# Conv taps handed out behind the projections' banks, and the conv normalisation as a step behind the last projection

## The chip, the cores and the metric

The kernel runs on one core of a Trainium2 chip, as one launch. The metric is the device time of one execution in microseconds. The core's engines each work through their own instruction stream in order: PE multiplies matrices, DVE and POOL work on vectors, ACT evaluates functions and makes scaled copies, SP's queue issues DMAs. An instruction that waits holds up all that stands behind it on its engine.

## The reference, cut to what matters

One layer over 1024 tokens of width 1024, all in float32. One projection of the normalised input feeds three groups of heads, whose outputs are joined, projected and added to the input; a gated feed-forward network follows.

```python
h = rms_norm(x, norm_mix[i])
proj = h @ w_in[i]
p_conv, p_nsa, p_rwkv = jnp.split(proj, splits, axis=-1)
y_conv = conv_mixer(p_conv, ...)
y_nsa = nsa_mixer(p_nsa, ...)
y_rwkv = rwkv7_mixer(p_rwkv, ...)
mix = jnp.concatenate([y_conv, y_nsa, y_rwkv], axis=-1)
x = x + mix @ w_out[i]
...
def conv_mixer(p, dw_w, dw_b, ln_g, ln_b):
    u, gate = jnp.split(p, 2, axis=-1)
    y = u * jax.nn.sigmoid(gate)
    y = causal_dwconv(y, dw_w, dw_b)     # 31 taps, 256 channels
    y = layer_norm(y, ln_g, ln_b, LN_EPS)
    return jax.nn.silu(y)
```

The attention group has compressed, selected and windowed keys. The RWKV group is a recurrence over the tokens, done in chunks, each of which needs a small triangular system solved.

## The kernel before, in words

Float32 products are made of three matmuls: both factors are split into a high and a low part, and `mm3` (L229) issues high by high, high by low and low by high. A weight block arrives by DMA as `wraw`; ACT writes its high part `whi` (L120) and DVE the difference `wlo` (L121). `proj_T` makes one block of 128 projection columns: two halves of 512 tokens, 24 matmuls each into one PSUM bank, and a `consume` function that reads the bank.

A framework puts the engines' instructions in order before the run: it takes them in program order as their priority and moves one ahead where an engine would otherwise wait. Steps of the recurrence are issued at high priority. Stage 1 is written by a string of steps:

```python
steps="lora r0 S00 conv taps V00 S01 keys q C00 V01 r1a cmp0 r1b cmp1 r1c S10 C01 V10 S11 C10 V11 C11"
```

`lora`, `r0`, `r1a` to `r1c` are projections for the recurrence (two pairs of heads, 0 and 1), `conv` those of the convolution (its gated input is `cy`, written at L257), `keys` and `q` those of the attention, `cmp0` and `cmp1` the compressed keys. S, V and C with two digits are the recurrence for a pair of heads and a half of the tokens:

- S prepares the operands (L430 to L478 on DVE, L446 and L474 on PE), multiplies them (L493, masked by DVE at L497 into `GA` and `GR`), sends `GA` through DRAM (`dn`, L503, and back into `sN`, L506), and then solves small triangular systems on POOL: 31 pairs of a product `sx` (L528) and a sum into `sT` (L530). DVE copies the result transposed (`sTT`, L532), and SP stores both (`dt`, `dtt`, L534 and L535). The next substitution begins with a copy into `sT` (L523), which must wait for those stores.
- V loads the result (`DF`, L543) and completes the solution with small matmuls (L550 and on).
- C walks through the eight chunks, each needing the state of the one before: L591, L596, L609 and L611 on PE, with DVE's work between them.

`taps` is `conv_rest`: 31 taps over two halves of 128 channels. For the first half DVE makes each tap in one instruction of 128x1024 (L270 for the first, L272 for the others, accumulator `cacc`). For the second half ACT scales (`ctap`, L278) and POOL adds (L274, L279), in pieces of 512 tokens. Behind the taps stands the layer normalisation over channels, for each half of the tokens: sums over partitions by matmuls (L284, L294, L303, into `tr` banks), DVE and ACT work, and four stores to `md` (L311).

Behind stage 1 comes the attention, first on POOL with copies of `kcmp`, `vcmp`, `gates` and `cval` (L669) and masks (L661, L663). Each of its tiles loads queries (`q`, L826, and `QS`, L831 and L832) and begins with matmuls on `kcmp` (L839) and on the keys (L893, L894); L918 are its first transposes.

Of the kernel before, what the change touches and what calls it, by code (L numbers as in the profile page):

```python
# [10 lines left out]
AF = mybir.ActivationFunctionType  # L11
ALU = mybir.AluOpType
AX = mybir.AxisListType
PSUM = bass.MemoryType.PSUM
T = 1024
D = 1024
P = 128


class K:  # L20
    def __init__(self, tc, a, out, ctx, bufs=None):
# [3 lines left out]
                      mm=3, tr=2, av=1, rw=2, mm1=2, tr1=2, pm=2, early="00 01", ga=2, gb=1, gc=1, y=16, r4=15, ta=3, tb=4, mid=2, de=dict(S3="gpsimd", T3="vector", T1="gpsimd", T2="gpsimd", T4="vector", S1="gpsimd", S2="gpsimd", S4="gpsimd"), order=(7, 6, 5, 4, 0, 3, 2, 1), sc=0, pk=1280, st="sync", last=5, sub="gpsimd",  steps="lora r0 S00 conv taps V00 S01 keys q C00 V01 r1a cmp0 r1b cmp1 r1c S10 C01 V10 S11 C10 V11 C11", both=0, cm="gpsimd", rpu=(), wo="vector", tap=(0, 31), vt="cv", vs="vector", va={1: (0, 1), 3: (2, 3), 5: (4, 5), 7: (6, 7)}, vq="sync", vl=1, vw=1, t1=("pm", "tr1"), into={6: (6, 2), 4: (4, 2), 3: (3, 1), 2: (2, 1), 1: (1, 1), 0: (0, 1)})  # L25
# [209 lines left out]
    def proj_T(self, cols, hT, consume, n=P, tag="mm1", halves=(0, 1)):  # L235

        hi, lo = self.wload(cols if isinstance(cols, list) else [cols], n)
        for half in halves:
            pt = self.bank(tag)
            self.mm3(pt[:n], [(hi[k], lo[k], hT[0][half][k], hT[1][half][k]) for k in range(8)])  # L240
            consume(half, pt)

# [17 lines left out]

    def conv_rest(self):
        nc = self.nc
        acc = [self.t4(name="cacc")[:, 0:T] for _ in range(2)]
        for j in range(2):
            y, t = self.cy[j], acc[j]
            m = self.B["tap"][j]
            for d in range(31):
                w = self.cw[:, j, d:d + 1]
                if d >= m and d == 0:
                    nc.vector.tensor_scalar(t, y[:, 0:T], w, self.cb[:, j:j + 1], op0=ALU.mult, op1=ALU.add)  # L270
                elif d >= m:
                    nc.vector.scalar_tensor_tensor(t, y[:, d:d + T], w, t, op0=ALU.mult, op1=ALU.add)  # L272
                elif d == 0:
                    nc.gpsimd.tensor_scalar(t, y[:, 0:T], w, self.cb[:, j:j + 1], op0=ALU.mult, op1=ALU.add)  # L274
                else:
                    for o in (0, 512):
                        z = self.xt([P, 512], "cv", name="ctap")
                        nc.scalar.activation(z, y[:, o + d:o + d + 512], AF.Copy, scale=w)  # L278
                        nc.gpsimd.tensor_tensor(t[:, o:o + 512], t[:, o:o + 512], z, op=ALU.add)  # L279
        for half in range(2):  # L280
            sl = slice(half * 512, half * 512 + 512)
            pm = self.bank("tr1")
# [21 lines left out]
            for j in range(2):  # L304
                z = self.xt([P, 512], "cv", name="cz")
# [967 lines left out]
    def build(self):  # L1273
        order = self.B["order"]
        nc, a = self.nc, self.a
# [7 lines left out]
        hT = self.T_tiles("hT", (self.x, "hx", self.B["hx"]))  # L1283
# [21 lines left out]
        us = {}  # L1305

# [9 lines left out]
        def chain(j, h):  # L1316
            with self.tc.high_priority(offset=100000):
                self.rwkv_chain(us[j, h])
        steps = dict(lora=lambda: self.rwkv_lora(hT), keys=lambda: self.attn_keys(hT), q=lambda: self.attn_q(hT),
                     cmp=lambda: self.attn_cmp(hT), conv=lambda: self.conv_proj(hT), taps=self.conv_rest, r0=lambda: self.rwkv_proj(0, hT),  # L1320
                     r1=lambda: self.rwkv_proj(1, hT), cmp0=lambda: self.attn_cmp(hT, (0,)), cmp1=lambda: self.attn_cmp(hT, (1,)),
                     r1a=lambda: self.rwkv_proj(1, hT, (0,)), r1b=lambda: self.rwkv_proj(1, hT, (1,)), r1c=lambda: self.rwkv_proj(1, hT, (2,)))
# [80 lines left out]
```

## Time and profile before

| | us |
|---|---|
| median of the three runs shown | 1532.06 |
| lowest and highest of them | 1527.68, 1541.17 |
| the profiled execution, its own time | 1533.06 |
| span of its trace | 1531.3 |

The profiled execution lies 1.00 us above the median, and 1.8 us of it lie outside the span. In the trace stage 1 ends at about 385 us, the attention and its surroundings fill the time to about 715, the output projection to about 835, and the feed-forward network the rest. All positions below are microseconds from the start of the span.

### The profile page before, as it was taken

How to read it: one execution, taken by the hardware profiler on the slowest of the kernel's cores; microseconds unless marked ns; L12 is line 12 of the kernel's file. 1: busy time of each engine (PE TensorE's matmuls, PEld its weight loads, DVE VectorE, ACT ScalarE, POOL GpSimd, SP SyncE). 2: the span in 40 equal slices, each digit the busy share in tenths (PEclk: the TensorE clock that was granted, in tenths of full speed). 3: DMA queues.
4: the chain of work that ended last, by engine and by line, in shares of the span. 5: the costliest groups of instructions: out<-in, count | busy, mean ns of one | idle time of the engine just before them, and what ended most of it. 6: DMA issues, size and time to landing. Idle time of an engine off the chain costs nothing.

```text
span 1531.3 us, 22605 instructions
## 1 busy us (share of the span) xinstructions
PE 1431.6 (93%) x8025; PEld 1135.8 (74%) x8025; DVE 1042.6 (68%) x2193; ACT 684.2 (45%) x1361; POOL 488.6 (32%) x585
## 2 busy tenths in 40 slices
PE   6999679999799999998899999999999999897897
PEld 5887457777677777775687788888888887685686
DVE  6247695453586778587267767767767668979976
ACT  6432354534266567677133534334433333343453
POOL 1004887910420050001001223323323315849820
PEclk9999787989799999999999999999999999998999
DMA  6142223433710112114522122222222229163302
GB/s 188 37 120 56 52 83 87 144 93 108 193 32 15 32 39 64 55 39 129 179 90 76 55 69 83 89 77 83 77 89 83 67 93 375 43 203 121 117 1 110
DMA packets 182916, 143.41 MB, mean 94 GB/s; under 512 B 53715, under 2 KB 143124, under 8 KB 182804
## 3 DMA queue, kind: packets, MB, share of 16 engines
q1 hardware_dynamic: 182804, 141.98, 30.5%
q8 instruction: 63, 1.03, 0.3%
q14 instruction: 49, 0.40, 0.1%
HBM read 103.92 MB, written 38.01 MB: 93 GB/s over the span
## 4 chain that ended last, share of the span: by engine, by line
PE 75%; DVE 11%; DMA 5%; POOL 3%; issue 2%; ACT 1%; SPq 1%; DVEq 0%; POOLq 0%; ACTq 0%
PE mm L229 13%; PE gb L229 12%; PE ga L229 9%; PE rw L229 8%; PE gc L229 8%; PE tr L918 5%; PE av L926 4%; DVE sp L121 4%; PE tr L229 3%; PE mm L893 2%; PE mm L894 2%; POOL sT L530 1%; POOL sx L528 1%; PE pm L493 1%; DVE cacc L272 1%
## 5 line engine op out<-in xcount | busy, mean ns | idle before, releaser
L229 PE MATMUL mm<-hT,whi 128*128 128x512 f32 x608 | 204.8, 418 | 0.0
L229 PE MATMUL mm<-hT,wlo 128*128 128x512 f32 x304 | 127.8, 422 | 20.3 <-DVE wlo L121 20.3
L229 PEld LDWEIGHTS mm<-hT,whi 128*128 128x128 f32 x608 | 120.2, 200 | 29.4 <-issue 1.6
L1050 POOL TENSOR_TENSOR S<-wraw,wr 128x512 f32<-128x512 f32 x22 | 28.5, 1297 | 257.9 <-DVE or L107 96.1
L921 ACT ACTIVATE pT<-tr 128x512 f32<-128x512 f32 (+1 forms) x152 | 80.0, 537 | 62.6 <-PE tr L918 61.3
L926 PE MATMUL av<-pT,V 128*64 128x128 f32 x1056 | 95.2, 286 | 4.0 <-ACT pT L921 3.9
L279 POOL TENSOR_TENSOR cacc<-cacc,ctap 128x512 f32<-128x512 f32 x60 | 91.1, 1542 | 17.7 <-ACT ctap L278 17.5
L229 PE MATMUL rw<-sp,sp 128*128 128x512 f32 x330 | 90.0, 397 | 7.1 <-DVE sp L121 6.6
L918 PE MATMUL tr<-idn,pp 128*128 128x128 f32 x528 | 89.6, 288 | 0.1
L229 PEld LDWEIGHTS mm<-hT,wlo 128*128 128x128 f32 x304 | 60.8, 200 | 38.6 <-DVE wlo L121 21.4
L229 PE MATMUL tr<-sp,sp 128*128 128x512 f32 x330 | 88.4, 395 | 0.0
L229 PE MATMUL rw<-woh,mix 128*128 128x512 f32 x240 | 78.9, 405 | 6.4 <-DVE xn L976 5.2
L926 PEld LDWEIGHTS av<-pT,V 128*64 128x64 f32 x1056 | 59.2, 136 | 28.9 <-issue 11.0
L229 PEld LDWEIGHTS rw<-sp,sp 128*128 128x128 f32 x330 | 62.6, 191 | 22.6 <-DVE sp L121 8.8
L893 PE MATMUL mm<-KH,QS 128*128 128x512 f32 (+2 forms) x192 | 74.1, 394 | 4.0 <-DMA QS<-qd 2.5
L918 PEld LDWEIGHTS tr<-idn,pp 128*128 128x128 f32 x528 | 55.7, 141 | 28.6 <-issue 27.3
L121 DVE TENSOR_TENSOR sp<-b,sp 128x512 fp32r<-128x512 f32 x60 | 65.5, 1104 | 13.4 <-ACT sp L120 13.3
L229 PEld LDWEIGHTS tr<-sp,sp 128*128 128x128 f32 x330 | 63.1, 191 | 13.4
L849 POOL TENSOR_TENSOR cmp<-cmp,cmx 128x512 f32<-128x512 f32 (+7 forms) x8 | 5.4, 680 | 206.2 <-DVE cmx L847 137.0
L120 ACT ACTIVATE whi<-wraw 128x512 fp32r<-128x512 f32 x55 | 34.6, 628 | 78.7 <-PE mm L229 60.3
L121 DVE TENSOR_TENSOR wlo<-wraw,whi 128x512 fp32r<-128x512 f32 x55 | 42.3, 771 | 34.9 <-ACT whi L120 34.8
L528 POOL TENSOR_TENSOR sx<-sN,sT 128x60 f32<-128x60 f32 (+24 forms) x124 | 43.8, 353 | 65.4 <-DMA sN<-dn 57.0
(460 smaller groups left out, 3846.3 us busy)
## 6 DMA issues: line engine op xcount, KB each, us to landing
wr<-in_ffn_w_gate_dram SPq DMA_DIRECT2D x44, 256.0 KB
wraw<-in_ffn_w_up_dram SPq DMA_DIRECT2D x44, 256.0 KB
pd<-prod SPq DMA_DIRECT2D x44, 256.0 KB
ta<-pd SPq DMA_DIRECT2D x33, 256.0 KB
wraw<-in_w_in_dram SPq DMA_DIRECT2D x30, 256.0 KB
tb<-in_ffn_w_down_dram SPq DMA_DIRECT2D x22, 256.0 KB
rb<-in_ffn_w_down_dram SPq DMA_DIRECT2D x20, 256.0 KB
qd<-ev SPq DMA_DIRECT2D x16, 256.0 KB
```

Of the source, the lines that this page charges most:

```text
L120: self.nc.scalar.activation(hi, src, AF.Copy)
L121: getattr(self.nc, eng).tensor_tensor(lo, src, hi.bitcast(F32), op=ALU.subtract)
L229: mm = lambda l, r, **k: self.nc.tensor.matmul(out, l, r, skip_group_check=more, **k)
L272: nc.vector.scalar_tensor_tensor(t, y[:, d:d + T], w, t, op0=ALU.mult, op1=ALU.add)
L279: nc.gpsimd.tensor_tensor(t[:, o:o + 512], t[:, o:o + 512], z, op=ALU.add)
L528: v_.tensor_tensor(x, N[:, q, q + 1:32].unsqueeze(2).to_broadcast([P, n, w]), Tm[:, q, 0:w].unsqueeze(1).to_broadcast([P, n, w]), op=ALU.mult)
L893: pe.matmul(pts[g][:, 0:n], QS[:, r, g, :], KH[g][hf][:, ks], start=True, stop=False)
L894: pe.matmul(pts[g][:, 0:n], QS[:, r, g, :], KL[g][hf][:, ks], start=False, stop=True)
L918: pe.transpose(pt[:, o:o + P], Ps[g][:, kt * P:kt * P + P], self.idn)
L921: s.activation(pT[:, 0:n], pt[:, 0:n], AF.Copy)
L926: pe.matmul(av[g * 64:g * 64 + 64, r * P:r * P + P], self.V[kk // 2][:, kk % 2, vo + g * 64:vo + g * 64 + 64], pT[:, o:o + P], start=first ...
L1050: gp.tensor_tensor(t, x, y, op=op)
```

## The change

The taps of both channel halves become a list `self.fill` of 62 small functions. `proj_T` calls up to three of them behind each `consume`, that is, behind each bank of every projection that follows `taps` in the string. What is left of the list is called at the new step `cend`, which then does the normalisation. `cend` stands behind `r1c` and ahead of S10; the normalisation stood within `taps`. Each of the list's functions has the same instructions as before; the two channel halves now alternate, the second first. Line numbers behind `proj_T` grow by 3 and behind the taps by 11: the copy `sTT` at L532 is L543 after, the substitution at L528 and L530 is L539 and L541, L669 is L680, L839 is L850, L550 is L561, the taps at L270 and L272 are L273 and L275.

```diff
@@ -22,7 +22,7 @@
...
-                      steps="lora r0 S00 conv taps V00 S01 keys q C00 V01 r1a cmp0 r1b cmp1 r1c S10 C01 V10 S11 C10 V11 C11", both=0,
+                      steps="lora r0 S00 conv taps V00 S01 keys q C00 V01 r1a cmp0 r1b cmp1 r1c cend S10 C01 V10 S11 C10 V11 C11", both=0, drip=3,
...
@@ -239,6 +239,9 @@
             pt = self.bank(tag)
             self.mm3(pt[:n], [(hi[k], lo[k], hT[0][half][k], hT[1][half][k]) for k in range(8)])
             consume(half, pt)
+            for _ in range(self.B["drip"]):
+                if self.fill:
+                    self.fill.pop(0)()
 
 
     def conv_proj(self, hT):
@@ -258,25 +261,33 @@
             self.proj_T(w[:, j * P:(j + 1) * P], hT, cu)
             self.cy.append(y)
 
+    def conv_taps(self):
+
+        nc = self.nc
+        self.cacc = [self.t4(name="cacc")[:, 0:T] for _ in range(2)]
+
+        def tap(d, j):
+            y, t, w = self.cy[j], self.cacc[j], self.cw[:, j, d:d + 1]
+            if d >= self.B["tap"][j]:
+                if d == 0:
+                    nc.vector.tensor_scalar(t, y[:, 0:T], w, self.cb[:, j:j + 1], op0=ALU.mult, op1=ALU.add)
+                else:
+                    nc.vector.scalar_tensor_tensor(t, y[:, d:d + T], w, t, op0=ALU.mult, op1=ALU.add)
+            elif d == 0:
+                nc.gpsimd.tensor_scalar(t, y[:, 0:T], w, self.cb[:, j:j + 1], op0=ALU.mult, op1=ALU.add)
+            else:
+                for o in (0, 512):
+                    z = self.xt([P, 512], "cv", name="ctap")
+                    nc.scalar.activation(z, y[:, o + d:o + d + 512], AF.Copy, scale=w)
+                    nc.gpsimd.tensor_tensor(t[:, o:o + 512], t[:, o:o + 512], z, op=ALU.add)
+        self.fill = [lambda d=d, j=j: tap(d, j) for d in range(31) for j in (1, 0)]
+
     def conv_rest(self):
         nc = self.nc
-        acc = [self.t4(name="cacc")[:, 0:T] for _ in range(2)]
-        for j in range(2):
-            y, t = self.cy[j], acc[j]
-            m = self.B["tap"][j]
-            for d in range(31):
-                w = self.cw[:, j, d:d + 1]
-                if d >= m and d == 0:
-                    nc.vector.tensor_scalar(t, y[:, 0:T], w, self.cb[:, j:j + 1], op0=ALU.mult, op1=ALU.add)
-                elif d >= m:
-                    nc.vector.scalar_tensor_tensor(t, y[:, d:d + T], w, t, op0=ALU.mult, op1=ALU.add)
-                elif d == 0:
-                    nc.gpsimd.tensor_scalar(t, y[:, 0:T], w, self.cb[:, j:j + 1], op0=ALU.mult, op1=ALU.add)
-                else:
-                    for o in (0, 512):
-                        z = self.xt([P, 512], "cv", name="ctap")
-                        nc.scalar.activation(z, y[:, o + d:o + d + 512], AF.Copy, scale=w)
-                        nc.gpsimd.tensor_tensor(t[:, o:o + 512], t[:, o:o + 512], z, op=ALU.add)
+        for f in self.fill:
+            f()
+        self.fill = []
+        acc = self.cacc
         for half in range(2):
             sl = slice(half * 512, half * 512 + 512)
             pm = self.bank("tr1")
@@ -1303,6 +1314,7 @@
         self.attn_params()
         g2 = self.g2
         us = {}
+        self.fill = []
 
         def start(j, h):
             with self.tc.high_priority(offset=100000):
@@ -1317,7 +1329,7 @@
             with self.tc.high_priority(offset=100000):
                 self.rwkv_chain(us[j, h])
         steps = dict(lora=lambda: self.rwkv_lora(hT), keys=lambda: self.attn_keys(hT), q=lambda: self.attn_q(hT),
-                     cmp=lambda: self.attn_cmp(hT), conv=lambda: self.conv_proj(hT), taps=self.conv_rest, r0=lambda: self.rwkv_proj(0, hT),
+                     cmp=lambda: self.attn_cmp(hT), conv=lambda: self.conv_proj(hT), taps=self.conv_taps, cend=self.conv_rest, r0=lambda: self.rwkv_proj(0, hT),
                      r1=lambda: self.rwkv_proj(1, hT), cmp0=lambda: self.attn_cmp(hT, (0,)), cmp1=lambda: self.attn_cmp(hT, (1,)),
                      r1a=lambda: self.rwkv_proj(1, hT, (0,)), r1b=lambda: self.rwkv_proj(1, hT, (1,)), r1c=lambda: self.rwkv_proj(1, hT, (2,)))
         for st in self.B["steps"].split():
```

On DVE, around the copy `sTT` of S00 (L532), the taps (L272) stand ahead of it before:

```order
L272 SCALAR_TENSOR_TENSOR cacc_1587<-cy_1389,par,cacc_1587 128x1024 x3
L424 SCALAR_TENSOR_TENSOR cum_2032<-rst,lw_2025 128x512
L272 SCALAR_TENSOR_TENSOR cacc_1587<-cy_1389,par,cacc_1587 128x1024
L432 TENSOR_SCALAR lw_2025<-rk_2015,par 128x512
L430 COPY rPC_2038<-Pt_2034 128x8
L461 TENSOR_TENSOR rP_2078<-rr_2016,Pt_2034 128x512
L257 SCALAR_TENSOR_TENSOR cy_1521<-ev_1455,mm_279_1535 128x512
L272 SCALAR_TENSOR_TENSOR cacc_1587<-cy_1389,par,cacc_1587 128x1024
L532 COPY sTT<-sT 128x256
L121 TENSOR_TENSOR wlo_2255<-wraw_2252,whi_2254 128x512
```

The same place of DVE after, from the write of `cy` (L260) that precedes `sTT` (L543) to the first tap (L273):

```order
L260 SCALAR_TENSOR_TENSOR cy_1521<-ev_1455,mm_279_1535 128x512
L543 COPY sTT<-sT 128x256
L121 TENSOR_TENSOR wlo_1931<-wraw_1928,whi_1930 128x512
L450 TENSOR_SCALAR rn_305_1723<-pm_1718 128x8
L106 TENSOR_SCALAR rs_t_307_1726<-rn_305_1723 128x8
L109 TENSOR_SCALAR rs_h_308_1729<-rn_305_1723 128x8
L107 TENSOR_SCALAR rrn_1725<-rs_t_307_1726 128x8
L260 SCALAR_TENSOR_TENSOR cy_1521<-ev_1456,mm_280_1561 128x512
L114 TENSOR_TENSOR rs_t_307_1726<-rrn_1725 128x8
L121 TENSOR_TENSOR wlo_1937<-wraw_1934,whi_1936 128x512
L273 TENSOR_SCALAR cacc_1587<-cy_1389,par 128x1024
```

All of the taps that stood ahead of `sTT` (15, with the first at L270) stand behind it now, from the first on; the 31 of them end among the weights of `q`, before those of the recurrence.

On POOL, at the end of stage 1, before: the attention's copies (L669) and masks (L661, L663), then the first product of S10's substitution (L528).

```order
L669 COPY kcmp_4457<-kcmp 128x128
L669 COPY vcmp_4459<-vcmp 128x128
L669 COPY gates_4461<-gates 128x192
L669 COPY cval_4463<-cval 128x1
L661 MEMSET msel 128x640
L661 MEMSET mwin 128x640
L661 MEMSET mcmp 128x120
L663 AFFINE_SELECT msel<-msel 128x640
L663 AFFINE_SELECT mwin<-mwin 128x640
L663 AFFINE_SELECT mcmp<-mcmp 128x120
L663 AFFINE_SELECT mwin<-mwin 128x640
L528 TENSOR_TENSOR sx<-sN,sT 128x31
```

The same place of POOL after: the last steps of S10's substitution (L539, L541), the copy into `sT` (L534) and the attention's copies (L680) and masks (L672, L674).

```order
L555 MEMSET sN 32x16x32
L541 TENSOR_TENSOR sT<-sT,sx 128x8
L534 COPY sT<-sI 128x256
L680 COPY kcmp_4457<-kcmp 128x128
L680 COPY vcmp_4459<-vcmp 128x128
L680 COPY gates_4461<-gates 128x192
L680 COPY cval_4463<-cval 128x1
L672 MEMSET msel 128x640
L672 MEMSET mwin 128x640
L672 MEMSET mcmp 128x120
L674 AFFINE_SELECT msel<-msel 128x640
```

The attention's copies and masks stood ahead of S10's 62 substitution steps and stand behind them now, and behind the next copy into `sT`.

On PE, at the first matmul of the attention (L839), before:

```order
L493 MATMUL rw_3514<-rP_3468,BK_3472 128x64 x4
L493 MATMUL rw_3514<-rP_3468,BK_3475 128x64 x4
L839 MATMUL mm_4546<-kcmp_4457,q_808_4539 128x128 x3
L517 MATMUL rw_3542<-idn,VAc_3409 128x128 x4
L839 MATMUL mm_4546<-kcmp_4457,q_808_4539 128x128
L893 MATMUL mm_4566<-KH_4511,QS_4541 128x256
L894 MATMUL mm_4566<-KL_4517,QS_4541 128x256
L517 MATMUL rw_3548<-idn,BK_3472 128x128 x4
L893 MATMUL mm_4567<-KH_4514,QS_4541 128x256
```

The same place of PE after, from the last steps of C01 (L602, L620, L622) to the attention's first matmuls (L850, L904):

```order
L602 MATMUL rw_3719<-rH_738,AT_1755 64x128
L620 MATMUL rw_3641<-VA_1840,GR_1817 64x64
L622 MATMUL rw_3641<-rH_738,rP_1754 64x64
L620 MATMUL rw_3641<-VA_1840,GR_1819 64x64
L622 MATMUL rw_3641<-rH_738,rP_1754 64x64
L850 MATMUL mm_4546<-kcmp_4457,q_808_4539 128x128 x4
L904 MATMUL mm_4566<-KH_4511,QS_4541 128x256
L905 MATMUL mm_4566<-KL_4517,QS_4541 128x256
```

Before, the first matmuls on `kcmp` follow directly on S10's products at L493, and the chain C01 runs among the attention's matmuls. After, the whole of C01 (its last step is shown) and the matmuls of the normalisation stand ahead of them. On SP's queue the loads of `q` and `QS` stood among S10's stores of `dn`, and stand behind its load of `DF` now.

## Rows read from the trace of the kernel before

**Rows 1.** The page, part 1: busy time, share of the span, instructions.

```profile
PE 1431.6 (93%) x8025; PEld 1135.8 (74%) x8025; DVE 1042.6 (68%) x2193; ACT 684.2 (45%) x1361; POOL 488.6 (32%) x585
```

**Rows 2.** Windows: stretch, length, busy PE, PEld, DVE, ACT, POOL, PEclk, DMA share, GB/s.

```profile
170.00:213.00 43.00, 34.10 (x232) 26.44 (x233) 41.97 (x41) 18.89 (x30) 31.55 (x21) 0.80 0.36 83
213.00:264.00 51.00, 48.00 (x227) 37.70 (x227) 34.05 (x41) 26.30 (x43) 41.23 (x33) 0.80 0.31 91
300.00:360.00 60.00, 60.00 (x376) 47.20 (x374) 26.31 (x83) 20.18 (x41) 8.35 (x30) 0.86 0.31 81
385.00:403.00 18.00, 13.95 (x69) 12.18 (x69) 8.65 (x18) 1.46 (x4) 7.76 (x11) 0.60 0.88 248
403.00:425.00 22.00, 18.39 (x106) 14.66 (x106) 14.25 (x56) 8.88 (x19) 14.45 (x44) 0.86 0.45 111
500.00:680.00 180.00, 179.32 (x1637) 135.59 (x1636) 135.87 (x520) 119.40 (x280) 25.45 (x71) 1.00 0.16 45
```

**Rows 3.** DVE timeline: start, us, line, op, tiles [idle before <- releaser].

```profile
170.06 0.70 DVE L532 COPY sTT<-sT 128x256 f32<-128x256 f32 x1 [14.71 <-POOL sT L530]
```

**Rows 4.** Timeline of PE from the same moment on.

```profile
171.40 0.80 PE L229 MATMUL mm<-hT,wlo 128*128 128x512 f32 x1 [12.82 <-DVE wlo L121]
...
176.82 1.21 PE L550 MATMUL rw<-DF,GA 32*32 32x32 f32 x32
```

**Rows 5.** Timeline of POOL in S00's substitution.

```profile
136.59 1.21 POOL L528 TENSOR_TENSOR sx<-sN,sT 128x29 f32<-128x29 f32 x1
...
155.61 0.29 POOL L528 TENSOR_TENSOR sx<-sN,sT 128x60 f32<-128x60 f32 x1
...
169.82 0.20 POOL L530 TENSOR_TENSOR sT<-sT,sx 128x8 f32<-128x8 f32 x1
...
174.50 0.77 POOL L523 COPY sT<-sI 128x256 f32<-128x256 f32 x1 [3.90 <-DMA dt<-sT]
```

**Rows 6.** Windows, DVE busy on L272; then tile cacc, ns min/median/max.

```profile
130.00:155.00 25.00, 17.60 (x14) 1.00 0.25 64
170.00:213.00 43.00, 26.48 (x16) 0.80 0.36 83
...
L272 DVE SCALAR_TENSOR_TENSOR cacc<-cy,par,cacc x30: 1255/1285/2386, 130.9 to 213.0; 128x1024 f32<-128x1024 f32 x30
```

**Rows 7.** Windows of PE on tile tr, and on tile rw.

```profile
296.00:357.00 61.00, 9.93 (x51) 0.86 0.31 85
...
412.00:470.00 58.00, 12.59 (x103) 1.00 0.15 32
```

**Rows 8.** Timeline of POOL at the end of stage 1.

```profile
384.97 2.47 POOL L669 COPY kcmp<-kcmp 128x128 f32<-128x128 f32 x1 [49.07 <-PE mm L229]
...
392.03 0.73 POOL L663 TENSOR_SCALAR_AFFINE_SELECT mwin<-mwin 128x640 f32<-128x640 f32 x1
407.50 0.24 POOL L528 TENSOR_TENSOR sx<-sN,sT 128x31 f32<-128x31 f32 x1 [14.74 <-DMA sN<-dn]
...
433.18 0.33 POOL L530 TENSOR_TENSOR sT<-sT,sx 128x8 f32<-128x8 f32 x1
440.21 0.79 POOL L523 COPY sT<-sI 128x256 f32<-128x256 f32 x1 [6.71 <-DMA dt<-sT]
```

**Rows 9.** Timeline of PE at the same place.

```profile
381.90 0.60 PE L446 MATMUL rw<-idn,cum 128*128 128x128 f32 x4
...
402.76 1.62 PE L839 MATMUL mm<-kcmp,q 128*128 128x128 f32 x6 [0.42 <-DMA q<-qd]
...
412.92 0.43 PE L591 MATMUL rw<-rH,AT 128*64 128x128 f32 x2
...
418.25 0.43 PE L591 MATMUL rw<-rH,AT 128*64 128x128 f32 x2
```

**Rows 10.** Timeline of SP's queue there: DMA issues.

```profile
398.63 0.57 SPq L826 DMA_DIRECT2D q<-qd  x1
...
440.10 0.34 SPq L543 DMA_DIRECT2D DF<-dt  x1
```

More of the change, by code (lines that the diff above doesn't have):

```diff
@@ L24, in __init__ @@
                       QS=2, pp=6, q8=2, pT=5, xn=8, h2=14, graw=2, prod=4, ft=4, u=4, wr2=4, wfh=3, wfl=3, S=2, p1=2, om=6, grow=2, pre=2, ap=(), wf=("own", "wf", "om"), hd=("vector",) * 4, tq=((0, 1, 2, 3),), ttag=("tr", "rw"),
-                      mm=3, tr=2, av=1, rw=2, mm1=2, tr1=2, pm=2, early="00 01", ga=2, gb=1, gc=1, y=16, r4=15, ta=3, tb=4, mid=2, de=dict(S3="gpsimd", T3="vector", T1="gpsimd", T2="gpsimd", T4="vector", S1="gpsimd", S2="gpsimd", S4="gpsimd"), order=(7, 6, 5, 4, 0, 3, 2, 1), sc=0, pk=1280, st="sync", last=5, sub="gpsimd",  steps="lora r0 S00 conv taps V00 S01 keys q C00 V01 r1a cmp0 r1b cmp1 r1c S10 C01 V10 S11 C10 V11 C11", both=0, cm="gpsimd", rpu=(), wo="vector", tap=(0, 31), vt="cv", vs="vector", va={1: (0, 1), 3: (2, 3), 5: (4, 5), 7: (6, 7)}, vq="sync", vl=1, vw=1, t1=("pm", "tr1"), into={6: (6, 2), 4: (4, 2), 3: (3, 1), 2: (2, 1), 1: (1, 1), 0: (0, 1)})
+                      mm=3, tr=2, av=1, rw=2, mm1=2, tr1=2, pm=2, early="00 01", ga=2, gb=1, gc=1, y=16, r4=15, ta=3, tb=4, mid=2, de=dict(S3="gpsimd", T3="vector", T1="gpsimd", T2="gpsimd", T4="vector", S1="gpsimd", S2="gpsimd", S4="gpsimd"), order=(7, 6, 5, 4, 0, 3, 2, 1), sc=0, pk=1280, st="sync", last=5, sub="gpsimd",  steps="lora r0 S00 conv taps V00 S01 keys q C00 V01 r1a cmp0 r1b cmp1 r1c cend S10 C01 V10 S11 C10 V11 C11", both=0, drip=3, cm="gpsimd", rpu=(), wo="vector", tap=(0, 31), vt="cv", vs="vector", va={1: (0, 1), 3: (2, 3), 5: (4, 5), 7: (6, 7)}, vq="sync", vl=1, vw=1, t1=("pm", "tr1"), into={6: (6, 2), 4: (4, 2), 3: (3, 1), 2: (2, 1), 1: (1, 1), 0: (0, 1)})
         self.B.update(bufs or {})
```

## Prediction

> **What bounds the kernel now.** I read the page first: PE is busy 93% of the span, DVE 68%, POOL 32% [rows 1], so time is to be found only where PE waits or runs at a lower clock. The windows say where that is. The attention leaves none: from 500 to 680 PE is busy 179.32 of 180 us at a clock of 1.00. The stretch from 170 to 264 is different: PE is busy 34.10 of 43 and 48.00 of 51 us at clock 0.80, and at its start DVE is full, 41.97 of 43. So is the seam between stage 1 and the attention: PE lacks 4 of 18 us and then 3.6 of 22, at clocks of 0.60 and 0.86 [rows 2]. The change touches these two places; the rest is the same work in the same order.
>
> The timelines then tell who ends the waits. At 171.40 PE has waited 12.82 us for a `wlo` from DVE [rows 4]. DVE had not been working on it: it stood 14.71 us at the copy `sTT`, until POOL's substitution S00 ended [rows 3]. POOL took 19.0 us for the 20 instructions from the 5th to the 25th of the 62 (136.59 to 155.61), 0.95 each, and 14.2 us for the 37 that followed, 0.38 each [rows 5]; DVE was making its first taps until 155.35, and none after. One tap beside this costs 17.60/14 = 1.26 us [rows 6]. So the taps slowed the substitution, and that is what the reader is to see in front.
>
> **Front: the taps leave the substitution.** By the order none stands ahead of `sTT` now. At 0.38 apiece the 20 slow instructions take 7.7 us, 11.3 less, and S00 ends at 158.7. DVE is free then, and PE has just reached the waiting matmul: of the 12.82 us some 1.5 stay. The next thing that could be late is the solve (L550, after L561), which came 7.0 us after the last substitution step [rows 4, 5], hence at 165.7. In the order 23 matmuls of `keys` stand ahead of it behind the first `wlo`, where there were 12; those 12 took 5.4 us, so 23 cover it. **Gain 11.3 us at this point.**
>
> **Front: the taps come back on DVE.** The 14 taps and the first one, which were hidden ahead of 155, now run behind 158.7, beside POOL's adds. There 16 taps took 26.48 us, 1.66 each [rows 6]; 15 of them add about 24 us. The bounds are the price alone, 1.26, and the highest of the 30, 2.386 [rows 6]: 18 and 34 us (rounded, with the shorter first tap). I take 1.66, the mean of the nearest stretch. DVE did 76.0 us of work between 170 and 264 [rows 2]; with the taps it is 100 (94 to 110), and from 158.8 it ends at 259 (253 to 269) even with no wait. PE, 11.3 us ahead, would ask for the last weights of `q` at 253. DVE becomes the bound there, and of the 11.3 us **about 5 stay (between -5 and +11).**
>
> The reason for the dearer taps shows as a price in the rows, 1.26 alone and up to 2.386 beside POOL. The Trainium skill, "SBUF — State Buffer", section "Who interferes with whom", has a rule that speaks against this change: a DVE instruction with two SBUF inputs and a GpSimd instruction that reads SBUF exclude each other, and the loser is blocked for the whole of the other. By it a tap would wait out an entire add each time, which the highest tap bears out and the mean of 1.66 doesn't; by the rule the upper bound is the likely value.
>
> **The normalisation leaves the projections.** Its matmuls are PE's work on the `tr` banks from 296 to 357, 9.93 us [rows 7]. It was on PE's path (60.00 of 60 busy [rows 2]), so the last projection ends 9.9 us earlier, and the work has to be done behind it. In the same stretch the clock is 0.86, worth 8.4 us if it were 1.00; no row tells how much of that the normalisation caused. Bounds 0 and 8.4, I take 4, half. With the 5 above, the projections end 9 us earlier from front and clock together, and 18.9 in all: T, the end of r1c, moves from 385 [rows 8] to about 366.
>
> **Seam: the attention waits for S10.** Before, POOL made the attention's copies and masks right at T, in 7.8 us, then waited for S10's `sN`, began at T+22.5 and ended at T+48.5; its next copy into `sT` waited 6.71 us more for the stores [rows 8]. PE began the attention at 402.76, T+17.8 [rows 9], with the `q` that SP had issued at 398.63 [rows 10]. In the order after, POOL's copies and masks stand behind S10's substitution and that copy; SP's loads of `q` and `QS` stand behind the load of `DF`, which also waits for the stores (440.10, 6.6 us after the substitution [rows 8, 10]). So the attention now hangs on the end of the whole of S10:
>
> - S10's first matmul, L446, was at 381.90, T-3 [rows 9]; its counterpart now stands behind the last projection, so S10 is 3 us later against T: substitution from T+25.5.
> - The substitution took 26.0 us [rows 8], with the attention's first POOL work among its steps. That now follows it, so I take 24, the 62 steps at the 0.38 us that they cost alone [rows 5]: it ends at T+49.5.
> - Stores and `DF`: T+56. Two more loads and then `q`, which took 4.1 us from issue to use [rows 9, 10]: the first matmul on `kcmp` at about T+61.4. POOL's path is no later: T+56.2, the copy 0.8, `kcmp` 2.5, so T+59.5; the last mask at T+65 against DVE's first need a few us behind the matmul.
> - C01 stands ahead of it too. Two of its steps lie 5.33 us apart among the attention's work [rows 9]; eight take 43, and from T+18 they end at T+61. They fill the wait and don't lengthen it.
>
> The attention so begins 43.6 us later relative to T (bounds 36, if the emptier DMA queues shorten S10's way through DRAM, and 48, if DVE's share of the normalisation gets ahead of S10's). What fills the gap on PE: the normalisation, counted already, and C01. On `rw` PE worked 12.59 us from 412 to 470 [rows 7]; less the three matmul groups of S10's solve at about 1.21 each [rows 4] that is 9.0 us, no longer in the attention. Of it 2.2 us (two of eight steps) lay where PE had idle time anyway [rows 2], so 6.8 count.
>
> **The sum.** -9.9 (normalisation away) - 9 (front, clock) + 43.6 (later start) - 6.8 (C01 done) = +17.9 us. On the profiled execution's 1533.06 that is 1551.0; it lies 1.0 above the median of the runs shown, so I forecast **1550 us**. Behind the seam nothing changes, and the attention, with PE full, has no slack to win the delay back. With the bounds of front and clock (-5 to +19) and start (36 to 48) it goes from 1532 to 1568.
>
> **Rivals.**
>
> - *Front gives back nearly as much* (within 1%). If a tap beside the adds costs 1.4 rather than 1.66, DVE is done at 255, the waits for `wlo` shrink, and with them part of the idle time of 11.9 us between 170 and 264 and of the clock at 0.80. With 24 us from front and clock instead of 9 the sum is +3: 1535. For it: three quarters of that idle time lie in the stretch in which DVE is full. Against it: DVE's load grows.
> - *Faster: DVE is never late.* If PE gets every weight in time from 158 to 264, it gains 11.3 of the stall, the other 11.9 idle us, 16 us from a clock of 1.00 in place of 0.80 (20% of 82 busy us), and the 8.4 from 300 on: 47.6, and the sum is -21: 1511. The point from which it decides is a gain of 42 us in front. Against it stands that POOL still has the second channel half's adds to do beside the taps.
> - *DVE is blocked by each add.* With 2.386 us a tap, DVE ends `q`'s weights at 269 or later, PE waits at each of them, nothing comes back from the clock, and the front loses 10 instead of gaining 9: 1569. For it: DVE was at 41.97 of 43 us with 16 taps, and now has 31. This is the case of the page's rule named above.
> - *The taps aren't paced.* "Three behind a bank" sets a priority, not a time: by the order all 31 of DVE's are issued before the weights of `q` end. Had they been spread to the end of stage 1, DVE would not bind and the front would keep 11 instead of 5: 1544. The order speaks against it, and its time is inside the forecast.
>
> **How the numbers follow.** Forecast (1541 to 1560) 0.52, front gives back 0.26, DVE blocked 0.16, faster 0.06. About 1% is what a measurement of this kernel can tell from no change; its bounds are 1516.7 and 1547.4. Slower by more holds two thirds of the forecast's case and all of the blocked one, 0.51; faster by more the last rival and a little of the second, 0.07; within 1% the rest, 0.42. The range of 1530 to 1571 leaves out the faster case, the far end of the blocked one and the lower part of the second.
>
> **What would show it.** Right: S00's instructions at 0.38 and `sTT` at about 159; PE's stall there under 3 us; taps near 1.7 and some above 2.3 between 160 and 260; r1c ending 15 to 25 us earlier; POOL's `kcmp` copy right behind S10's substitution and its wait for `dt`; PE idle by 25 us or more ahead of its first matmul on `kcmp`, which comes 60 us behind T; the attention as long as before. Wrong: masks that are done before S10's substitution begins, a first `kcmp` matmul within 30 us of T, or waits for `wlo` that vanish altogether.

## The result, and the profile after

The changed kernel takes 1552.9 us, the median of executions from 1552.19 to 1555.51, against 1533.28 for the kernel before beside it: a ratio of 1.0127 (95% interval 1.008 to 1.0174). The forecast was 1550. The profiled execution has a span of 1551.7 us, 20.4 more than before.

The page, part 1, of the kernel after, which answers to [rows 1]: busy time is about the same, PE's 9 us more.

```profile
PE 1440.6 (93%) x8025; PEld 1134.9 (73%) x8025; DVE 1054.4 (68%) x2193; ACT 684.1 (44%) x1361; POOL 486.2 (31%) x585
```

The same windows as [rows 2], columns as there:

```profile
170.00:213.00 43.00, 29.33 (x238) 23.44 (x239) 38.16 (x32) 23.67 (x39) 37.32 (x24) 0.82 0.25 69
213.00:264.00 51.00, 43.11 (x197) 32.63 (x196) 50.44 (x43) 19.99 (x31) 46.45 (x31) 0.78 0.27 75
300.00:360.00 60.00, 60.00 (x399) 47.46 (x398) 19.66 (x46) 22.64 (x50) 7.00 (x25) 1.00 0.36 95
385.00:403.00 18.00, 16.97 (x82) 12.69 (x81) 9.51 (x18) 3.50 (x7) 5.16 (x15) 0.61 0.42 119
403.00:425.00 22.00, 16.97 (x94) 11.84 (x95) 12.74 (x44) 2.22 (x4) 14.78 (x49) 0.72 0.13 29
```

In front PE is busy less than before in both stretches: 13.7 us idle in the first and 7.9 in the second, where before lacked 8.9 and 3.0. DVE is the full engine now from 213 to 264, 50.44 of 51. From 300 to 360 the clock is 1.00 where it was 0.86.

DVE's timeline in front, answering to [rows 3], and the last step of the normalisation, which the last store takes out:

```profile
161.09 0.70 DVE L543 COPY sTT<-sT 128x256 f32<-128x256 f32 x1 [3.21 <-POOL sT L541]
...
183.26 2.36 DVE L275 SCALAR_TENSOR_TENSOR cacc<-cy,par,cacc 128x1024 f32<-128x1024 f32 x1
185.54 0.68 DVE L697 TENSOR_TENSOR ev<-mm,ev 128x512 fp32r<-128x512 f32 x1
...
424.05 0.69 DVE L321 SCALAR_TENSOR_TENSOR cth<-cth,cz 128x512 f32<-128x512 f32 x1
```

The taps by tile, ns min/median/max (answers to [rows 6]):

```profile
L275 DVE SCALAR_TENSOR_TENSOR cacc<-cy,par,cacc x30: 1271/1958/2393, 165.8 to 262.1; 128x1024 f32<-128x1024 f32 x30
```

The copy `sTT` is no longer held 14.71 us but 3.21, nine us earlier. The 30 taps now have a median of 1.958 us, where it was 1.285 [rows 6], and `ev` (L697), DVE's reading of a `keys` bank, stands behind them.

PE's timeline, from the front, through the normalisation (L295, L305 and L314, and of its second round L314 alone), to the attention's first matmuls; it answers to [rows 4, 9]:

```profile
186.28 1.22 PE L229 MATMUL mm<-hT,whi 128*128 128x512 f32 x2 [8.68 <-DVE ev L697]
...
372.32 0.39 PE L229 MATMUL mm<-hT,wlo 128*128 128x512 f32 x1
...
373.00 1.98 PE L295 MATMUL tr<-cacc,ones 128*128 128x512 f32 x4
...
377.03 1.89 PE L305 MATMUL tr<-ones,csq 128*128 128x1 f32 x14 [0.22 <-ACT csq L300]
...
389.60 2.07 PE L314 MATMUL tr<-cdg,ones 128*128 128x512 f32 x2
...
413.84 2.08 PE L314 MATMUL tr<-cdg,ones 128*128 128x512 f32 x2
...
427.38 0.42 PE L622 MATMUL rw<-rH,rP 128*64 128x64 f32 x2
...
432.57 2.04 PE L850 MATMUL mm<-kcmp,q 128*128 128x128 f32 x8 [4.77 <-DMA q<-qd]
```

POOL at the same place (answers to [rows 8]):

```profile
396.75 0.24 POOL L539 TENSOR_TENSOR sx<-sN,sT 128x31 f32<-128x31 f32 x1 [61.50 <-DMA sN<-dn]
...
421.32 0.20 POOL L541 TENSOR_TENSOR sT<-sT,sx 128x8 f32<-128x8 f32 x1
427.89 0.40 POOL L534 COPY sT<-sI 128x256 f32<-128x256 f32 x1 [6.37 <-DMA dt<-sT]
428.22 0.29 POOL L680 COPY kcmp<-kcmp 128x128 f32<-128x128 f32 x1
```

And SP's queue (answers to [rows 10]):

```profile
421.55 1.27 SPq L545 DMA_DIRECT2D dt<-sT  x2
...
426.94 0.54 SPq L322 DMA_DIRECT2D md<-cth  x1
427.79 0.34 SPq L554 DMA_DIRECT2D DF<-dt  x1
...
429.30 0.58 SPq L837 DMA_DIRECT2D q<-qd  x1
```

The projections end at T = 372.7, 12.1 us earlier than before. The first matmul on `kcmp` comes at 432.57, T+59.9, where it came at T+17.9 (T was 384.8): 41.9 us later against T. The output projection ends at 850.6 in place of 828.1, so between the two 7.3 us come back, and the feed-forward network is 2.1 shorter: -12.1 + 41.9 - 7.3 - 2.1 = +20.4.

What the reader should see in these fences is that **three chains end together**: S10's substitution with its stores (427.9), C01 (427.8), and the normalisation, whose last store goes out at 426.94. What that store takes out was ready at 424.74, and it stands behind S10's stores in SP's queue; `q` stands behind the load of `DF`, which needs those stores. So S10 ends last here, and the two others are within some 3 us of it. The normalisation was about 10 us of PE's work before and is 14.7 here, at a granted clock of 0.68. It is a chain through PE, DVE, ACT and SP, stands behind S10's products on PE at each turn, and runs from T to T+54.

### The profile page after: what moved, and what is told of

The parts are those of the page before. It is cut to its first block, busy times and chain, and to the rows that moved or that the text cites. A ratio compares the mean times of both kernels' runs of the same rounds, so it can differ in the third digit from the quotient of the medians.

```text
span 1551.7 us, 22605 instructions
## 1 busy us (share of the span) xinstructions
PE 1440.6 (93%) x8025; PEld 1134.9 (73%) x8025; DVE 1054.4 (68%) x2193; ACT 684.1 (44%) x1361; POOL 486.2 (31%) x585
## 3 DMA queue, kind: packets, MB, share of 16 engines
q1 hardware_dynamic: 182804, 141.98, 30.5%
## 4 chain that ended last, share of the span: by engine, by line
PE 71%; DVE 12%; POOL 5%; DMA 4%; issue 4%; ACT 2%; SPq 1%; DVEq 0%; POOLq 0%; ACTq 0%
PE gb L229 12%; PE mm L229 11%; PE rw L229 9%; PE ga L229 8%; PE gc L229 8%; PE av L937 5%; PE tr L929 4%; DVE sp L121 4%; PE tr L229 3%; PE mm L904 2%; PE mm L905 2%; POOL sT L541 2%; POOL sx L539 2%; DVE cacc L275 1%; DVE tb L1135 1%
## 5 line engine op out<-in xcount | busy, mean ns | idle before, releaser
L229 PE MATMUL mm<-hT,whi 128*128 128x512 f32 x608 | 201.5, 413 | 12.1 <-DVE ev L697 11.6
L539 POOL TENSOR_TENSOR sx<-sN,sT 128x60 f32<-128x60 f32 (+24 forms) x124 | 43.7, 352 | 163.2 <-DMA sN<-dn 154.8
L904 PE MATMUL mm<-KH,QS 128*128 128x512 f32 (+2 forms) x192 | 75.7, 399 | 1.0 <-DVE mx L908 0.9
L281 ACT ACTIVATE ctap<-cy,par 128x512 f32<-128x512 f32 x60 | 43.2, 722 | 52.8 <-POOL cacc L282 51.4
L908 DVE CUSTOM_DVE_ANT_0 pp<-mm,msel 128x512 f32<-128x512 f32 (+3 forms) x96 | 51.4, 552 | 22.3 <-PE mm L905 14.1
```

The lines of the kernel that those rows point to most:

```text
L229: mm = lambda l, r, **k: self.nc.tensor.matmul(out, l, r, skip_group_check=more, **k)
L539: v_.tensor_tensor(x, N[:, q, q + 1:32].unsqueeze(2).to_broadcast([P, n, w]), Tm[:, q, 0:w].unsqueeze(1).to_broadcast([P, n, w]), op=ALU.mult)
L904: pe.matmul(pts[g][:, 0:n], QS[:, r, g, :], KH[g][hf][:, ks], start=True, stop=False)
L908: v.tensor_tensor_reduce(Ps[g][:, ka - lo_k:kb - lo_k], pts[g][:, o:o + kb - ka], mask(ka, kb), 1.0, 3.4e38, ALU.add, ALU.min, mx[:, g, c: ...
```

## Experiments

All edits are made to the changed kernel; only what differs from it is shown. Executions of the kernel before lie between 1523.9 and 1547.2 us, so the time of a single execution tells little below some 10 us, and such a run is read by the positions in its trace.

**The normalisation alone is moved** (the taps stay where they were before):

```diff
-        self.fill = [lambda d=d, j=j: tap(d, j) for d in range(31) for j in (1, 0)]
+        for j in range(2):
+            for d in range(31):
+                tap(d, j)
```

> The kernel before with the normalisation alone moved to cend behind r1c; all taps are issued at their old place, 15 of DVE's ahead of sTT. Theory (seam): PE's stall of some 13 us at S00 is there as before, r1c ends 10 to 18 us earlier than before, the first kcmp matmul comes about 60 us behind it, and the time is 1547 to 1557 us. Rival (front): without the taps beside POOL's adds there is nothing to lose, 1520 to 1530 us.

Measured: 1551.7 us, ratio 1.0122 (1.007 to 1.0174). PE's timeline of this kernel:

```profile
173.15 0.80 PE L229 MATMUL mm<-hT,wlo 128*128 128x512 f32 x1 [12.74 <-DVE wlo L121]
...
368.91 0.39 PE L229 MATMUL mm<-hT,wlo 128*128 128x512 f32 x1
...
429.58 2.04 PE L852 MATMUL mm<-kcmp,q 128*128 128x128 f32 x8 [5.13 <-DMA q<-qd]
```

The stall is back and nearly the whole loss is here without the taps' move: the loss belongs to the normalisation's place. T is 369.3, 15.5 us earlier than before and 3.4 earlier than with the taps moved.

**The taps alone are moved** (the normalisation soon behind the taps):

```diff
-steps="... keys q C00 V01 r1a cmp0 r1b cmp1 r1c cend S10 C01 ..."
+steps="... keys q cend C00 V01 r1a cmp0 r1b cmp1 r1c S10 C01 ..."
```

> The changed kernel with its step cend moved from behind r1c to behind q: the taps stand behind the substitution S00 as in the changed kernel, the normalisation is back among the projections, and in the order the attention's copies and masks stand ahead of S10's substitution again. Theory (the seam costs the time, the front about nothing): the first kcmp matmul comes within 25 us of the end of r1c, r1c ends at 383 to 391, and the time is 1531 to 1540 us. Rival (DVE's taps beside POOL's adds cost the time, the seam is filled): 1548 to 1555 us, with r1c ending 15 us or more later than in the kernel before.

Measured: 1540.58, ratio 1.0036 (1.0006 to 1.0065). PE:

```profile
406.80 1.65 PE L850 MATMUL mm<-kcmp,q 128*128 128x128 f32 x6
```

T is 386.1 and the attention begins at T+20.7, so the seam is near what it was before (T+17.9). The taps' move by itself wins nothing; the time is 0.6 us above the theory's span.

**The normalisation in the middle**, behind `cmp0`:

```diff
+steps="... r1a cmp0 cend r1b cmp1 r1c S10 C01 ..."
```

> The changed kernel with cend behind cmp0: in the order the last matmul of the normalisation stands near the end of r1c, and POOL's copy of kcmp stands behind 17 rows of S10's substitution, between the place of the kernel before and that of the changed one. Theory (the attention comes in the order behind the last piece of the normalisation, and what stands ahead of it by then on POOL, SP and PE sets its start): first kcmp matmul 30 to 40 us behind r1c's end, 1538 to 1547 us. Rival (front): as the changed kernel, 1549 to 1556 us.

Measured: 1528.64, ratio 0.9984 (0.9951 to 1.0017); T 376.5, the attention at T+30.4. The start fell in its span, the time came out 9 us under it.

**The same with the taps at their old place:**

```diff
+steps="... r1a cmp0 cend r1b cmp1 r1c S10 C01 ..."
...
+        for j in range(2):
+            for d in range(31):
+                tap(d, j)
```

> All taps at the place of the kernel before (15 of DVE's ahead of sTT), the normalisation alone at a step behind cmp0; in the order it stands at the end of r1c and the copy of kcmp ahead of S10's substitution. Theory (the loss of the change comes with the attention's place behind the normalisation's last piece, not with the normalisation's being late as such): start 18 to 25 us behind r1c's end, PE's stall of some 13 us at S00 as before, time 1526 to 1537 us. Rival (a late normalisation costs the time itself): 1542 us or more.

Measured: 1540.98, ratio 1.0047 (1.0018 to 1.0076), 4 us above the theory's span. T is 377.2 and the attention begins at 400.55, earlier than the 406.98 of the kernel with the taps moved as well. The time is lost behind: windows of this kernel within the attention.

```profile
510.00:530.00 20.00, 20.00 (x179) 15.58 (x179) 15.62 (x57) 11.19 (x23) 0.00 (x0) 1.00 0.16 42
530.00:550.00 20.00, 20.00 (x106) 17.02 (x107) 8.63 (x23) 5.78 (x12) 7.11 (x22) 0.57 0.18 45
```

PE is busy in all 40 us, but from 530 on the granted clock is 0.57, for most of the time the lower of its two levels (1.2 and 2.4 GHz); the kernel before has 1.00 there. That is 20 x 0.43 = 8.6 us, if the work there goes by the clock. PE had been full at 1.00 ahead of the fall; what brought it on is not known from these rows. The taps-alone kernel has a smaller fall at the same place (0.66 from 540 to 550). The fall is not the whole loss: from the first `kcmp` matmul to the end of the output projection this kernel takes 436.0 us and the one with the taps moved as well 417.7; of the 18.2 us PE is idle for 5.6 (17.3 against 11.7).

**The substitution of S10 cut short**: does the attention hang on it?

```diff
-        for q in range(31):
+        for q in range(1 if (u.j, u.h) == (1, 0) else 31):
```

> The changed kernel with S10's substitution cut to its first pair of instructions (30 of 31 pairs are left out for this one step). POOL then reaches the attention's copies some 23 us earlier. Theory as forecast (the queue behind the substitution sets the start, C01 ahead on PE only fills the gap): the first kcmp matmul moves from 60 to about 37 us behind r1c's end, and the time falls by 15 to 23 us to about 1530 to 1538. Rival (C01, which ended 4.8 us ahead of the first kcmp matmul in the changed kernel, is just as late): the start moves by 5 us or less, 1546 to 1551 us.

Measured in a single execution: 1550.88. POOL, then PE, then SP of this kernel:

```profile
405.19 0.29 POOL L680 COPY kcmp<-kcmp 128x128 f32<-128x128 f32 x1
```

```profile
429.19 0.42 PE L622 MATMUL rw<-rH,rP 128*64 128x64 f32 x2
429.54 2.08 PE L850 MATMUL mm<-kcmp,q 128*128 128x128 f32 x8
```

```profile
421.55 4.17 SPq L322 DMA_DIRECT2D md<-cth  x2
425.76 0.58 SPq L837 DMA_DIRECT2D q<-qd  x1
```

POOL is done 23 us earlier and PE begins 3 us earlier. My theory fell: the rest stands at C01, whose last step (L622) PE has just ended, and behind the normalisation's stores, right behind which `q` goes out.

**C01 behind the solve V10**:

```diff
+steps="... r1c cend S10 V10 C01 S11 ..."
```

> The changed kernel with C01 behind V10 in the string: in the order PE's first kcmp matmul stands ahead of C01, on POOL and SP all is as in the changed kernel. Theory (POOL's and SP's queues set the start, C01 fills the gap with 6.8 us of worth): start still about 60 us behind r1c's end, time 1555 to 1563 us, 4 to 9 above the changed kernel. Rival (PE's own queue, C01, sets the start): the first kcmp matmul at 45 us or less, 1535 to 1548 us.

Measured: 1553.18, ratio 1.0118 (1.0072 to 1.0165). PE, then the normalisation's last step on DVE, then SP:

```profile
431.53 1.89 PE L561 MATMUL rw<-DF,GA 32*32 32x32 f32 x32 [18.66 <-DMA DF<-dt]
...
434.12 2.05 PE L850 MATMUL mm<-kcmp,q 128*128 128x128 f32 x8 [0.70 <-DMA q<-qd]
```

```profile
418.57 0.69 DVE L321 SCALAR_TENSOR_TENSOR cth<-cth,cz 128x512 f32<-128x512 f32 x1 [1.47 <-ACT cth L320]
```

```profile
429.22 0.34 SPq L554 DMA_DIRECT2D DF<-dt  x1
...
430.73 0.58 SPq L837 DMA_DIRECT2D q<-qd  x1
```

The attention begins where it did (T+60.0) with PE idle ahead of it, so C01 is not what sets it. The normalisation isn't either in this run, since its last step ended at 419.26 and only its store stands behind S10's in SP's queue. What is left is S10: its substitution ends at 423.0, its stores let `DF` go at 429.22, and `q` follows at 430.73. So with C01 out of the way **S10 alone holds the start**, as the prediction said. Yet leaving C01 for later cost nothing, where 4 to 9 us had been expected. The windows of the attention's end, first of before, then of after, then of this kernel, show why:

```profile
690.00:760.00 70.00, 58.41 (x363) 42.77 (x362) 33.55 (x123) 34.00 (x87) 4.60 (x5) 0.95 0.52 161
```

```profile
720.00:800.00 80.00, 72.10 (x476) 54.86 (x473) 36.31 (x138) 37.31 (x101) 1.82 (x4) 0.94 0.28 96
```

```profile
720.00:800.00 80.00, 76.94 (x445) 58.01 (x444) 43.07 (x144) 38.92 (x98) 3.48 (x4) 0.96 0.53 168
```

Between the attention and the output projection there is a hole: PE idle 11.6 us before, 7.9 after, 3.1 here. What is put off into the attention can be paid from it.

**Both at once**, the short substitution and C01 behind V10:

```diff
+steps="... r1c cend S10 V10 C01 S11 ..."
...
+        for q in range(1 if (u.j, u.h) == (1, 0) else 31):
```

> The changed kernel with both chains out of the way: S10's substitution cut to its first pair (30 of 31 pairs are left out) and C01 behind V10 in the string. Each of the two alone left the start and the time where they were. Theory (two chains of nearly the same length, POOL's and SP's queue behind the substitution and PE's C01, each cover for the other): the first kcmp matmul now comes 35 to 45 us behind r1c's end instead of 57 to 60, and the time is 1530 to 1542 us. Rival (a third thing, the loads of q or the normalisation, holds the start): start still past 52 us, 1547 us or more.

Measured in a single execution: 1548.39, the attention at T+61 (432.11). POOL's `kcmp` copy came at 403.6. SP, then PE:

```profile
422.08 5.11 SPq L322 DMA_DIRECT2D md<-cth  x2
427.24 0.58 SPq L837 DMA_DIRECT2D q<-qd  x1
```

```profile
431.52 0.66 PE L602 MATMUL rw<-rH,AT 128*64 128x128 f32 x2
432.11 2.08 PE L850 MATMUL mm<-kcmp,q 128*128 128x128 f32 x8
```

The start does not move, but the edit did not take C01 out of the way. With the short substitution V10's solve begins at 405.19, and the first steps of C01 (L602, four times from 422.40) stand ahead of the attention on PE; the first `kcmp` matmul follows the fourth without a wait. V10's solve stands ahead of the normalisation too, whose last step ends at 426.83 here and ended at 419.26 with C01 late alone; `q` goes out right behind its last store. So this run shows the normalisation's stores as near to the start as PE's queue, and does not part the two.

**The second token half's normalisation left out**, S10 and C01 whole:

```diff
+            if half:
+                for j in range(2):
+                    self.st.dma_start(self.md[:, j, sl], acc[j][:, sl])
+                continue
```

> The changed kernel with the normalisation of the second half of the tokens left out (those values are stored as the taps leave them); S10's substitution and C01 are whole, and the string is that of the changed kernel. In the order the attention's copies then stand behind 15 rows of S10's substitution, and PE's first kcmp matmul ahead of C01. Theory (the attention's place in all queues is behind the normalisation's last piece, its last store on SP included; S10 and C01 hold it up only because they get ahead of it by then): the first kcmp matmul comes 28 to 40 us behind r1c's end instead of 60, the time is 1526 to 1540 us. Rival (S10's substitution or C01 hold the start by themselves): 50 us or more, 1545 us or more.

Measured: 1527.52, ratio 0.9969 (0.9946 to 0.9991). PE, then POOL, then SP:

```profile
368.09 0.39 PE L229 MATMUL mm<-hT,wlo 128*128 128x512 f32 x1
...
399.02 0.91 PE L854 MATMUL mm<-kcmp,q 128*128 128x128 f32 x6 [0.98 <-DMA q<-qd]
```

```profile
398.57 0.29 POOL L684 COPY kcmp<-kcmp 128x128 f32<-128x128 f32 x1
```

```profile
390.31 4.52 SPq L326 DMA_DIRECT2D md<-cth  x2
394.88 0.58 SPq L841 DMA_DIRECT2D q<-qd  x1
```

The attention begins at T+30.5 while the substitution still runs (392.6 to 424.7) and C01 too. Half of the normalisation was 5 us of PE's work before; leaving it out gives 25. So neither S10 nor C01 holds the attention by its own length: in the changed kernel they hold it because it is queued behind them. Where it is queued follows the normalisation's last piece in this run: the loads on SP come right behind the last store, and POOL's copies stand among the substitution's steps. With the normalisation whole behind `cmp0` the loads come right behind its last store as well (`q` at 402.67). Why the framework ties the two is not shown by a row.

**The front: POOL's 60 adds left out.**

```diff
-                    nc.gpsimd.tensor_tensor(t[:, o:o + 512], t[:, o:o + 512], z, op=ALU.add)
```

> The changed kernel without POOL's 60 adds of the second channel half (that half's convolution is left out but for its first tap; ACT still makes the scaled copies). It measures what the adds cost the taps. Theory (taps are dear because of the adds, and DVE is then late with weights and with the evacuation of the banks of keys): the 30 taps take 1.25 to 1.35 us each instead of a median of 1.96, the last ends near 235 instead of 264, PE's waits for DVE between 170 and 264 fall from some 24 us to under 8, r1c ends 12 to 25 us earlier than 372.7. Rival (the number of taps alone fills DVE): the waits stay above 15 us and r1c ends less than 8 us earlier.

Measured in a single execution: 1508.07. The taps, and the first window:

```profile
L275 DVE SCALAR_TENSOR_TENSOR cacc<-cy,par,cacc x30: 1274/1284/2106, 161.9 to 232.2; 128x1024 f32<-128x1024 f32 x30
```

```profile
170.00:213.00 43.00, 43.00 (x307) 34.58 (x306) 36.98 (x54) 40.17 (x69) 0.00 (x0) 0.98 0.45 124
```

The taps fall to a median of 1.284 us and end at 233 rather than 264, PE is full, and T is 333.5, 39.2 earlier, more than the 12 to 25 expected. The order of the work behind differs here too, so the 39.2 is not the adds' price alone. The adds bound the front of the changed kernel, by holding DVE's taps or by keeping POOL busy until about 293; this run takes both away and does not part them.

**Each add replaced by two memsets** of the same tile, so that POOL is busy and only writes:

```diff
-                    nc.gpsimd.tensor_tensor(t[:, o:o + 512], t[:, o:o + 512], z, op=ALU.add)
+                    nc.gpsimd.memset(t[:, o:o + 512], 0.0)
+                    nc.gpsimd.memset(t[:, o:o + 512], 0.0)
```

> The changed kernel with each of POOL's 60 adds replaced by two memsets of the same tile (the second channel half's convolution is left out): POOL is about as busy, but only writes. Theory by the Trainium skill's rule (SBUF - State Buffer, Who interferes with whom: a DVE instruction with two SBUF inputs is held up by a GpSimd instruction that reads SBUF, not by one that only writes): the taps' median falls to 1.25 to 1.35 us, the last tap ends before 245, r1c ends 8 us or more earlier than 372.7. Rival (any work of POOL beside them makes the taps dear): the median stays above 1.6 us.

Measured in a single execution: 1547.92. DVE, by tile and in its timeline, then POOL's last memset of a long row:

```profile
L275 DVE SCALAR_TENSOR_TENSOR cacc<-cy,par,cacc x30: 1268/1279/1296, 162.9 to 269.0; 128x1024 f32<-128x1024 f32 x30
...
178.16 39.72 DVE L455 COPY cum<-rrn 128x512 f32<-128x512 f32 x1
```

```profile
217.00 0.60 POOL L283 MEMSET cacc<- 128x512 f32 x1
```

No tap is held: 1.296 at most. Only ten of the 30 ran beside memsets (four from 169.7 to 178.2, six behind 258), at 1.27 to 1.29 us; most of the others had POOL idle beside them. But another DVE instruction, the copy `cum`, was held: 39.72 us (0.41 in the changed kernel) while POOL ran some 85 memsets back to back, and it ended 0.3 us behind the last of them. PE waited 35.9 us for it. So T, 371.5, was hardly earlier, and the expected front gain could not be seen.

**Sixteen taps held back** until the sixth of the eight banks of `q` has been read, by a copy `cw2` of their weights that DVE makes there; the string is that of the taps alone:

```diff
-            y, t, w = self.cy[j], self.cacc[j], self.cw[:, j, d:d + 1]
+            y, t, w = self.cy[j], self.cacc[j], (self.cw2[:, d:d + 1] if j == 0 and d >= 15 else self.cw[:, j, d:d + 1])
...
+                if (j, half) == (2, 1):
+                    self.cw2 = self.small([P, 31], "cw2", bufs=1)
+                    nc.vector.scalar_tensor_tensor(self.cw2, t[:, 0:31], 0.0, self.cw[:, 0, :], op0=ALU.mult, op1=ALU.add)
```

> cend behind q as in the run with the early normalisation, and DVE's taps from the 16th on read their weights from a small copy that DVE makes only when the sixth bank of q has been read, so that they can't be issued sooner; nothing is left out. Theory (DVE is overloaded between 160 and 264 by taps beside adds, and half empty behind): PE's waits for DVE between 160 and 264 fall from some 24 us to under 10, r1c ends at 368 to 378 instead of 386, 1520 to 1530 us. Rival (the taps cost POOL and DVE the same wherever they stand beside adds, which go on to 290): r1c ends at 383 or later, 1535 us or more.

Measured: 1540.62, ratio 1.0032 (1.0003 to 1.0061), the same as the taps alone without it; T 389.5. PE is busy 49.43 of 51 us from 213 to 264, and behind that 31.43 of 36 (264 to 300) and 54.00 of 60 (300 to 360): the waits have only moved with the taps.

**The same with the normalisation behind `cmp0`:**

```diff
+steps="... r1a cmp0 cend r1b cmp1 r1c S10 C01 ..."
```

> The same gate on the taps with cend behind cmp0. In the order the normalisation ends near the end of r1c and POOL's copy of kcmp stands ahead of S10's substitution. Theory: the front gain of the gate and a start of the attention some 20 us behind r1c's end add up, 1513 to 1526 us. Rival (what the gate wins in front is lost to the normalisation's wait near the end): 1528 us or more.

Measured: 1531.48, ratio 0.9987 (0.9953 to 1.002), no gain over the same string without the hold; T 378.2. The profiled execution, 1537.29 us, has the fall of the clock as well: 0.56 from 530 to 540 and 0.59 to 550.

## Why the prediction was right, point by point

- **The attention waits behind the moved step: right in place and size.** Forecast 43.6 us later against T, measured 41.9; the first `kcmp` matmul at T+61.4 and T+59.9. POOL's copy stands right behind the wait for `dt`, as the prediction said. One of its signs failed: PE is idle for 14.9 us between T and that matmul, not 25; it worked 44.9 us there, at a granted clock of 0.66.
- **"The attention now hangs on the end of the whole of S10": right, but incomplete.** S10 does end last, and with C01 late it holds the start by itself (T+60.0). But C01 and the normalisation end within some 3 us of it: with the substitution cut the start moved only 3 us against T. With half of the normalisation left out it moved by 29. The prediction priced the normalisation as 9.9 us of PE's work and did not follow it as a chain through four engines, nor did it say that the normalisation's place is what puts the attention behind S10. How long this chain would take without S10's work ahead of it was not tried.
- **The normalisation leaves the projections: right.** With it alone moved T is 15.5 us earlier: 9.9 of work and, by difference, 5.6 for the clock (0.86 to 1.00 between 300 and 360), where 4 was taken.
- **The front, "about 5 stay": wrong, it was -3.4**, near the lower bound of -5. The stall at `wlo` did vanish and S00 ended at 161.1 (forecast 158.7; the substitution took 25.6 us and began 2.2 later). The 11.3 us came out (36.7 to 25.6), though [rows 5] were miscounted: between 136.59 and 155.61 lie 18 instructions at 1.06 us, not 20 at 0.95, and 39 follow at 0.36, which makes 12.5. But the term was sized by a tap of 1.66 us and the mean is 57.42/30 = 1.91, and it looked at weights only: the largest new wait is for `ev`, 8.68 us at 186.28, since DVE reads PE's banks behind the taps. The taps end at 264, where all of DVE's work up to there was forecast to end at 259.
- **DVE blocked by each add.** The highest tap is 2.393 us, and the mean lies between 1.28 and that; with POOL's adds gone the median is 1.284, and the ten taps beside memsets took 1.27 to 1.29. So the contention is with the adds. By the Trainium skill, "SBUF — State Buffer", section "Who interferes with whom", a DVE instruction with two SBUF inputs and a GpSimd one that reads SBUF exclude each other, and one that only writes is no hindrance: for the taps the traces agree, though a tap was held 0.63 us on the average (1.91 less 1.28), about half of an add's median of 1.378.
- **C01 done, -6.8: the size was near (7.3 came back), but it doesn't hang on C01 alone.** "Behind the seam nothing changes" and "no slack to win the delay back" were wrong: there is a hole ahead of the output projection, and with C01 put back into the attention 11 us came back from there, PE's idle time from the first `kcmp` matmul to 800 falling from 12.6 to 4.0 us. The granted clock in the attention can differ by 8.6 us as well.
- **The other rivals.** "DVE is never late" and "the front gives back nearly as much" fell: PE's idle time between 170 and 264 rose from 11.9 to 21.6 us. "The taps aren't paced" holds as a fact, since the 31 end by 264, ahead of the recurrence's projections; held back, they won nothing.
- **The sum: near, in part by luck.** T came 12.1 us earlier and not 18.9, so 6.8 were missing ahead of T. The seam (1.7 less than forecast), what came back behind it (0.5 more) and the feed-forward network (2.1 shorter) gave 4.3 of them back: 17.9 + 6.8 - 4.3 = 20.4.

No kernel here is clearly faster than the one before: the normalisation in the middle gives 0.9984 with an interval that holds 1, and the ones without half of it or without the adds do less work.

## What to carry to other kernels

A step that is moved behind the last large stage can take the next stage's place in the in-order queues with it, so follow it through all engines as a chain, to its last store, and not only by the bound engine's busy time. When several chains end within a few microseconds, removing one shows nothing; remove them together, see in the trace that each is really gone from ahead of the start, or shorten each until the start moves. Moving vector work off a stall gains little where its new place is beside an engine that contends with it and ahead of the reads that free PSUM banks.

## What the runs showed of the hardware

A DVE copy of 128x512 floats stood 39.72 us beside some 85 memsets on POOL, back to back, and 0.41 us otherwise, while the ten taps beside memsets took 1.27 to 1.29. POOL's small steps of the substitution took 1.06 us beside DVE's taps and 0.36 without [rows 5]; with the taps gone the whole took 25.6 us instead of 36.7. PE's granted clock fell to 0.57 for 20 us, from 530 to 550 in one of the kernels, in a stretch where PE was busy without a gap.
